# Feed-forward stage: squares on ScalarE, operands in PSUM, five pairs ahead, a second pair ahead in each down group, first token half finished first

## Chip, cores and metric

The kernel runs on one core of one Trainium2 chip. The metric is the device time of one execution in microseconds; the time before is the median of three runs, 2409.03 us (2401.53 to 2418.07).

## What is computed

A decoder layer over 1024 tokens of width 1024: two gated branches (a recurrent one and a dilated attention), cross-attention over 256 memory rows, a squared-ReLU feed-forward part and a final normalisation. The change touches the last two alone:

```python
u = rmsnorm(h, norm_ffn_g[l]) @ ffn_w1[l]                 # 1024 x 4096
h = h + (jnp.square(jax.nn.relu(u)) @ ffn_w2[l])
return rmsnorm(h, norm_final_g)
```

All of it is in fp32. A matmul with fp32-like precision is three matmuls: each operand is split into a high part `h` and a low remainder `l`, and `h*ah + h*al + l*ah` is summed in PSUM.

## The kernel before

Activations are kept transposed, `hT[d][half]`: 128 features by 512 tokens, two token halves. Both products of the feed-forward part are done with seven block products in place of eight (Strassen's method in Winograd's form). For an up **pair** (two blocks of 128 of the 4096 features; 16 pairs, `up_item`) the four weight blocks a0 to a3 and the sums made of them (`weights`, L1391: c3 = a2+a3, c2 = c3-a0, c4 = a0-a2, c6 = a1-c2) are multiplied with seven **combinations** of the normalised activations (`com[j]`, four pairs of tiles each). A product j is twelve matmuls of 512 columns (`seventh`, L1416) into one of four PSUM banks (`ms_tile`). `up_evac` (L1434) adds the seven results into the four blocks u11, u12, u21, u22, applies squared ReLU on VectorE (`squared`, L1428), forms the combinations that the down product needs (L1488 to L1491) and writes seven tiles per pair to DRAM (`uscr`). The down product runs in four **groups** g of 1024 features; a group has four items q (each two output blocks). At a group's first item `second` (L1539) loads the four tiles of each combination back (`ur`, six buffers, four of them shared with other tiles) and splits them: a cast on ScalarE, in three of four cases a copy of the high part into a PSUM tile (`split_psum`, `pacc`: two banks), and the low part on VectorE. `down_evac` (L1497) adds the seven results into `hT`, some of the additions on GpSimd.

A weight block is loaded by SyncE's queue (`f_raw`, six buffers), cast on ScalarE and its low half taken on GpSimd (`f_split`, L1379); four split blocks can wait for TensorE.

The seven combinations of the up product are made by `first_coms` (L1549): those of the first half (0 and 1) before the stage, 2 to 6 in the order 3, 4, 2, 5, 6 while the stage runs, on VectorE with casts on ScalarE. To have work meanwhile, `prologue` does products 0 and 1 of the first `PRO` = 3 pairs; what they give is kept in SBUF (product 0) and DRAM (the finished u11). `stream` (L1690) then goes through the items: product 0 of an item, product 5 of the previous one, product 1, product 6 of the previous one, and 2, 3, 4. Pairs of the prologue do 3, 4, 2. In the last group the outputs are finished (`finish`: four transposes, squares with a row sum on ScalarE, a multiplication by the final weight), and `last(half)` scales by the row norm and stores, 16 transfers of 256 KB on SyncE's queue. In the last item the order of the products is 2, 4, 5, 3, 6, and both calls of `last` come behind the sixth.

Each engine works through its instructions in one fixed order. The program's order is the order in which the generators above are advanced (`weave`, L151, deals steps of two streams out in proportion); the framework lays out the engines' queues at build time from that order, its own estimate of durations and the release of buffers, so an instruction whose inputs are early can stand ahead of ones that come before it in the program.

Of the kernel before, what the change touches and what calls it, by code (L numbers as in the profile page):

```python
# [41 lines left out]
def hybrid_layer(ctx, tc, x, mem, norm_mix_g, w_in, shift_mu, w0, w2, a0, a2, g2, k_k, k_a, r_k, gn_w, gn_b,  # L42
# [1336 lines left out]
    def f_split(raw):  # L1379
# [5 lines left out]
        nc.gpsimd.tensor_tensor(l, raw, h.bitcast(F32), op=ALU.subtract)  # L1385
# [5 lines left out]
    def weights(views, early=False):  # L1391
# [4 lines left out]
        def get(j):  # L1396
            if j < 2:
                return f_split(f_raw(views[j]) if early else a[j])
            if not c:
                c[3], c[2] = f_sum(), f_sum()  # L1400
                nc.vector.tensor_tensor(c[3], a[2], a[3], op=ALU.add)  # L1401
                nc.vector.tensor_tensor(c[2], c[3], a[0], op=ALU.subtract)
            if j in (2, 3):
                return f_split(c[j])
            if j == 4:
                c[4] = f_sum()
                nc.vector.tensor_tensor(c[4], a[0], a[2], op=ALU.subtract)
                w = f_split(c[4])
                c[6] = f_sum()
# [18 lines left out]
    def squared(dst, src):  # L1428
        nc.vector.scalar_tensor_tensor(dst, src, 0.0, src, op0=ALU.max, op1=ALU.mult)

    def add(dst, a, b, eng=None):
        (eng or nc.vector).tensor_tensor(dst, a, b, op=ALU.add)  # L1432

    def up_evac(p, st, j):  # L1434
# [8 lines left out]
        elif j == 1:  # L1443
            st["11"] = staged() if p >= PRO else bt.tile([P, H2], F32, tag="nt", name=nm("ua"))
            add(st["11"], st["a"], ps)
            if p >= PRO:
                squared(st["11"], st["11"])
            else:
                nc.scalar.activation(st["11"], st["11"], AF.Relu)
                nc.scalar.activation(st["11"], st["11"], AF.Square)  # L1450
            put(0, st["11"])
        elif p < PRO and j in (2, 3, 4):

            if j == 3:
                st["12"] = staged()
# [24 lines left out]
        elif j == 6:  # L1480
# [5 lines left out]
            squared(u12, u12)  # L1486
            t1, t2, t4 = [staged() for _ in range(3)]
            nc.vector.tensor_tensor(t1, u12, u11, op=ALU.subtract)  # L1488
            nc.vector.tensor_tensor(t2, u22, t1, op=ALU.subtract)
            nc.vector.tensor_tensor(u12, u22, u12, op=ALU.subtract)  # L1490
            nc.vector.tensor_tensor(t4, u21, t2, op=ALU.subtract)  # L1491
# [5 lines left out]
    def down_evac(g, q, st, j):  # L1497
        (h11, h12), (h21, h22) = [[hT[2 * q + e][half] for half in range(2)] for e in range(2)]
        ps = st["p", j]
        if j in (0, 2, 4):  # L1500
            t = staged()
            if j == 0:
                nc.scalar.copy(t, ps)
            else:
                add(t, st["t"], ps)
            st["t"] = t
        if j == 0:
            add(h11, h11, t, nc.vector)
        elif j == 1:
            add(h11, h11, ps)  # L1510
        elif j == 2:
            add(h12, h12, t, nc.gpsimd)
        if j == 4:
            add(h21, h21, t, nc.gpsimd)
            add(h22, h22, t, nc.vector)
# [224 lines left out]
```

## Time and profile before

| | us |
|---|---|
| median of three runs | 2409.03 |
| lowest, highest | 2401.53, 2418.07 |
| profiled execution | 2407.52 |
| its span, first to last instruction | 2405.8 |
| busy in the span: TensorE, VectorE, ScalarE, GpSimd | 2292.9, 1545.9, 1088.3, 889.4 |

The feed-forward stage is the last 686 us of the span (from about 1719.5 us); all matmuls of it have the lines L1422 to L1424. Matmuls are pipelined: the profile's duration of one is longer than the distance to the next, so the pace is read from counts. [...]

### The profile page before, as it was taken

What the parts mean: (1) busy time and instruction counts of PE and PEld (TensorE: products, weight loads), DVE (VectorE), ACT (ScalarE), POOL (GpSimd) and SP (SyncE); (2) the same over time, 40 slices, a digit from 0 to 9 for tenths busy, and PEclk for the clock granted to TensorE, in tenths of its full rate; (3) what the DMA queues carried; (4) which work ended last, traced back from release to release, by engine and by line L of the source; (5) the groups of instructions that cost most, each with busy time, mean ns of one, the idle gap of its engine ahead of it and who ended that gap; (6) DMA issues with size and microseconds to landing.
All of it is one profiled execution on the core that took longest, in us unless ns stands there. A gap on an engine that the chain in (4) does not pass through costs nothing. (4 is left out here: it accounts for less than half of the span.)

```text
span 2405.8 us, 47020 instructions
## 1 busy us (share of the span) xinstructions
PE 2292.9 (95%) x18645; PEld 1827.2 (76%) x18645; DVE 1545.9 (64%) x2735; ACT 1088.3 (45%) x2118; POOL 889.4 (37%) x737
## 2 busy tenths in 40 slices
PE   6999999999999999999999999999989999899997
PEld 5777777777777777777777888888768888678785
DVE  6638676786776722233474666345799898876685
ACT  5525645546455434333443445444432222565464
POOL 4321222222222223111245534423535554566664
PEclk9999999999999999999999999999999999999998
DMA  5221111111111123121245554223244444653352
GB/s 174 58 65 35 37 39 35 37 42 28 34 38 37 46 67 106 41 67 45 82 149 161 168 150 135 81 61 87 81 133 152 149 145 160 217 167 118 119 156 71
DMA packets 301619, 226.73 MB, mean 94 GB/s; under 512 B 16229, under 2 KB 252375, under 8 KB 301399
## 3 DMA queue, kind: packets, MB, share of 16 engines
q1 hardware_dynamic: 301111, 223.20, 30.6%
q8 instruction: 147, 2.41, 0.4%
q14 instruction: 73, 0.60, 0.1%
q10 hardware_dynamic: 288, 0.52, 0.1%
HBM read 169.99 MB, written 53.67 MB: 93 GB/s over the span
## 5 line engine op out<-in xcount | busy, mean ns | idle before, releaser
L143 PE MATMUL acc<-ah,wh 128*128 128x512 f32 (+1 forms) x1600 | 652.4, 408 | 8.4 <-DVE al L1266 2.9
L144 PE MATMUL acc<-al,wh 128*128 128x512 f32 (+1 forms) x1600 | 618.2, 386 | 2.8 <-POOL al L231 1.5
L145 PE MATMUL acc<-ah,wl 128*128 128x512 f32 (+1 forms) x1600 | 618.2, 386 | 0.4 <-POOL wl L112 0.4
L112 POOL TENSOR_TENSOR wl<-wr,wh 128x512 fp32r<-128x512 f32 x248 | 334.6, 1350 | 706.9 <-ACT wh L110 668.3
L143 PEld LDWEIGHTS acc<-ah,wh 128*128 128x128 f32 x1600 | 302.8, 189 | 76.3 <-issue 3.9
L145 PEld LDWEIGHTS acc<-ah,wl 128*128 128x128 f32 x1600 | 302.7, 189 | 62.5 <-POOL wl L112 1.0
L144 PEld LDWEIGHTS acc<-al,wh 128*128 128x128 f32 x1600 | 303.4, 190 | 50.9 <-POOL al L231 3.3
L110 ACT CAST wh<-wr 128x512 fp32r<-128x512 f32 (+1 forms) x296 | 179.6, 607 | 299.2 <-PE acc L144 186.1
L1423 PE MATMUL ms<-al,wh 128*128 128x512 f32 x768 | 304.5, 396 | 10.4 <-DVE al L1537 5.4
L1422 PE MATMUL ms<-ah,wh 128*128 128x512 f32 x768 | 304.4, 397 | 5.4 <-ACT ah L128 2.5
L1424 PE MATMUL ms<-ah,wl 128*128 128x512 f32 x768 | 302.3, 394 | 0.0
L1385 POOL TENSOR_TENSOR wl<-ws,wh 128x512 fp32r<-128x512 f32 x128 | 178.6, 1398 | 177.7 <-ACT wh L1384 149.6
L1385 POOL TENSOR_TENSOR wl<-sr,wh 128x512 fp32r<-128x512 f32 x96 | 140.4, 1465 | 113.7 <-ACT wh L1384 113.6
L1423 PEld LDWEIGHTS ms<-al,wh 128*128 128x128 f32 x768 | 145.2, 189 | 48.7 <-DVE al L129 9.5
L1422 PEld LDWEIGHTS ms<-ah,wh 128*128 128x128 f32 x768 | 145.1, 189 | 41.9 <-ACT ah L128 5.0
L1424 PEld LDWEIGHTS ms<-ah,wl 128*128 128x128 f32 x768 | 145.2, 189 | 31.9 <-POOL wl L1385 0.2
L1384 ACT CAST wh<-ws 128x512 fp32r<-128x512 f32 x128 | 79.0, 620 | 171.5 <-PE ms L1423 145.9
L1384 ACT CAST wh<-sr 128x512 fp32r<-128x512 f32 x96 | 59.5, 620 | 147.7 <-PE ms L1423 136.7
L937 DVE CUSTOM_DVE_ANT_0 sS<-pS,bias 128x128 f32<-128x128 f32 (+1 forms) x96 | 30.2, 349 | 113.5 <-PE pS L125 113.3
L399 ACT ACTIVATE gt<-acc 128x512 f32<-128x512 f32 x32 | 19.0, 594 | 127.1 <-PE acc L145 121.3
L942 ACT ACTIVATE sS<-sS,nm 128x128 f32<-128x128 f32 (+1 forms) x96 | 42.5, 443 | 75.2 <-DVE nm L940 72.1
L1432 DVE TENSOR_TENSOR sg<-sg,ms 128x512 f32<-128x512 f32 x70 | 47.7, 683 | 37.5 <-PE ms L1424 36.6
(420 smaller groups left out, 4048.3 us busy)
## 6 DMA issues: line engine op xcount, KB each, us to landing
sr<-in_ffn_w_dram SPq DMA_DIRECT2D x134, 256.0 KB
wr<-in_w_in_dram SPq DMA_DIRECT2D x120, 256.0 KB
ur<-uscr SPq DMA_DIRECT2D x112, 256.0 KB
uscr<-sg SPq DMA_DIRECT2D x93, 256.0 KB
gtscr<-gt SPq DMA_DIRECT2D x32, 256.0 KB
g<-gtscr SPq DMA_DIRECT2D x32, 256.0 KB
wr<-in_p_rwkv_dram SPq DMA_DIRECT2D x32, 256.0 KB
wr<-in_w_out_dram SPq DMA_DIRECT2D x32, 256.0 KB
```

Of the source, the lines that this page charges most:

```text
L110: nc.scalar.copy(h, raw)
L112: lo_eng.tensor_tensor(l, raw, h.bitcast(F32), op=ALU.subtract)
L143: mms.append(nc.tensor.matmul(ps, h, ah, start=(k == 0), stop=False))
L144: mms.append(nc.tensor.matmul(ps, h, al, start=False, stop=False))
L145: mms.append(nc.tensor.matmul(ps, l, ah, start=False, stop=(k == len(acts) - 1)))
L942: nc.scalar.activation(sS[:, h, lo:], sS[:, h, lo:], AF.Exp, bias=nm2[:, h:h + 1], scale=0.125, accum_out=Og[:, b, 130 + h:131 + h])
L1384: nc.scalar.copy(h, raw)
L1385: nc.gpsimd.tensor_tensor(l, raw, h.bitcast(F32), op=ALU.subtract)
L1422: nc.tensor.matmul(ps, h[:, k, :], ah, start=(k == 0), stop=False)
L1423: nc.tensor.matmul(ps, h[:, k, :], al, start=False, stop=False)
L1424: nc.tensor.matmul(ps, l[:, k, :], ah, start=False, stop=(k == 3))
L1432: (eng or nc.vector).tensor_tensor(dst, a, b, op=ALU.add)
```

## The change

The squares of up pairs become two ScalarE passes, Relu and Square. Weight sums c3 and c2 of the up pairs from 5 on and of the first three down groups are made in two PSUM banks (`f_psum`), and the low halves of those two are taken on VectorE; c4 becomes a3-c2, which is the same sum. The tiles b12, b2 and b of the evacuations stand in `pacc` banks, so that VectorE's sums there have one operand in PSUM, and the additions that GpSimd made in `down_evac` and `last` go to VectorE and ScalarE. `PRO` is 5; pairs 3 and 4 keep product 0 in DRAM and load it back for product 3 (`KEPT` = 3). In each down group products 0 and 1 of the second item (`ahead`) are done before products 2, 3, 4 of the first, from weight blocks loaded for that and loaded again later. In the last item (`final`) the order is 0, 5 of the item before, 1, 2, 4, 5, 6 of the item before, 3, 6, and `last(0)` stands ahead of product 6.

```diff
--- before.py
+++ after.py
@@ -1376,19 +1376,22 @@
         nc.sync.dma_start(t, ap)
         return t
 
-    def f_split(raw):
+    def f_split(raw, lo_eng=None):
         pool = wq[0] if wn[0] % 4 == 3 else wp
         wn[0] += 1
         h = pool.tile([P, 4, P], F32R, tag="wh", name=nm("wh"))
         l = pool.tile([P, 4, P], F32R, tag="wl", name=nm("wl"))
         nc.scalar.copy(h, raw)
-        nc.gpsimd.tensor_tensor(l, raw, h.bitcast(F32), op=ALU.subtract)
+        (lo_eng or nc.gpsimd).tensor_tensor(l, raw, h.bitcast(F32), op=ALU.subtract)
         return h, l
 
     def f_sum():
         return wrp[-1].tile([P, 4, P], F32, tag="wr", name=nm("ws"))
 
-    def weights(views, early=False):
+    def f_psum():
+        return fps.tile([P, 4, P], F32, tag="f", name=nm("wf"))
+
+    def weights(views, early=False, bank=False, held=False):
 
         a = [None if early else f_raw(v) for v in views]
         c = {}
@@ -1397,16 +1400,17 @@
             if j < 2:
                 return f_split(f_raw(views[j]) if early else a[j])
             if not c:
-                c[3], c[2] = f_sum(), f_sum()
+                c[3], c[2] = [f_psum() if bank else f_sum() for _ in range(2)]
                 nc.vector.tensor_tensor(c[3], a[2], a[3], op=ALU.add)
                 nc.vector.tensor_tensor(c[2], c[3], a[0], op=ALU.subtract)
             if j in (2, 3):
-                return f_split(c[j])
+                return f_split(c[j], nc.vector if bank else None)
             if j == 4:
+
                 c[4] = f_sum()
-                nc.vector.tensor_tensor(c[4], a[0], a[2], op=ALU.subtract)
+                nc.vector.tensor_tensor(c[4], a[3], c[2], op=ALU.subtract)
                 w = f_split(c[4])
-                c[6] = f_sum()
+                c[6] = staged().rearrange("p (k c) -> p k c", c=P) if held else f_sum()
                 nc.vector.tensor_tensor(c[6], a[1], c[2], op=ALU.subtract)
                 return w
             return f_split(a[3] if j == 5 else c[6])
@@ -1426,10 +1430,11 @@
                 yield
 
     def squared(dst, src):
-        nc.vector.scalar_tensor_tensor(dst, src, 0.0, src, op0=ALU.max, op1=ALU.mult)
-
-    def add(dst, a, b, eng=None):
-        (eng or nc.vector).tensor_tensor(dst, a, b, op=ALU.add)
+        nc.scalar.activation(src, src, AF.Relu)
+        nc.scalar.activation(dst, src, AF.Square)
+
+    def add(dst, a, b):
+        nc.vector.tensor_tensor(dst, a, b, op=ALU.add)
 
     def up_evac(p, st, j):
         def put(jj, t):
@@ -1441,17 +1446,18 @@
             st["a"] = bt.tile([P, H2], F32, tag="nt", name=nm("ua"))
             nc.scalar.copy(st["a"], ps)
         elif j == 1:
-            st["11"] = staged() if p >= PRO else bt.tile([P, H2], F32, tag="nt", name=nm("ua"))
+            st["11"] = staged() if p >= KEPT else bt.tile([P, H2], F32, tag="nt", name=nm("ua"))
             add(st["11"], st["a"], ps)
-            if p >= PRO:
-                squared(st["11"], st["11"])
-            else:
-                nc.scalar.activation(st["11"], st["11"], AF.Relu)
-                nc.scalar.activation(st["11"], st["11"], AF.Square)
+            if KEPT <= p < PRO:
+                put(1, st["a"])
+            squared(st["11"], st["11"])
             put(0, st["11"])
         elif p < PRO and j in (2, 3, 4):
 
             if j == 3:
+                if p >= KEPT:
+                    st["a"] = staged()
+                    nc.sync.dma_start(st["a"], uscr[(p * 7 + 1) * P:(p * 7 + 2) * P, :])
                 st["12"] = staged()
                 add(st["12"], st["a"], ps)
             elif j == 4:
@@ -1483,12 +1489,15 @@
                 nc.sync.dma_start(st["11"], uscr[p * 7 * P:(p * 7 + 1) * P, :])
             u11, u12, u21, u22 = st["11"], st["a"], st["21"], st["22"]
             add(u12, u12, ps)
-            squared(u12, u12)
+
+            b12, b2 = acc_tile(), acc_tile()
+            squared(b12, u12)
             t1, t2, t4 = [staged() for _ in range(3)]
-            nc.vector.tensor_tensor(t1, u12, u11, op=ALU.subtract)
-            nc.vector.tensor_tensor(t2, u22, t1, op=ALU.subtract)
-            nc.vector.tensor_tensor(u12, u22, u12, op=ALU.subtract)
-            nc.vector.tensor_tensor(t4, u21, t2, op=ALU.subtract)
+            nc.vector.tensor_tensor(t1, b12, u11, op=ALU.subtract)
+            nc.vector.tensor_tensor(u12, u22, b12, op=ALU.subtract)
+            nc.vector.tensor_tensor(b2, u22, t1, op=ALU.subtract)
+            nc.scalar.copy(t2, b2)
+            nc.vector.tensor_tensor(t4, u21, b2, op=ALU.subtract)
             put(3, t1)
             put(2, t2)
             put(4, u12)
@@ -1497,22 +1506,25 @@
     def down_evac(g, q, st, j):
         (h11, h12), (h21, h22) = [[hT[2 * q + e][half] for half in range(2)] for e in range(2)]
         ps = st["p", j]
-        if j in (0, 2, 4):
-            t = staged()
-            if j == 0:
-                nc.scalar.copy(t, ps)
-            else:
-                add(t, st["t"], ps)
-            st["t"] = t
         if j == 0:
-            add(h11, h11, t, nc.vector)
+            st["t"] = staged()
+            nc.scalar.copy(st["t"], ps)
+            add(h11, h11, ps)
         elif j == 1:
             add(h11, h11, ps)
         elif j == 2:
-            add(h12, h12, t, nc.gpsimd)
-        if j == 4:
-            add(h21, h21, t, nc.gpsimd)
-            add(h22, h22, t, nc.vector)
+
+            t = staged()
+            add(t, st["t"], ps)
+            st["t"] = t
+            b = acc_tile()
+            nc.scalar.copy(b, t)
+            add(h12, h12, b)
+        elif j == 4:
+            b = acc_tile()
+            add(b, st["t"], ps)
+            add(h21, h21, b)
+            add(h22, h22, b)
         if 3 in st["seen"] and 4 in st["seen"] and j in (3, 4):
             add(h22, h22, st["p", 3])
             add(h12, h12, st["p", 3])
@@ -1620,13 +1632,13 @@
         it["evac"](it["st"], j)
         yield
 
-    def item(views, evac, **kw):
-        return dict(st={}, w=weights(views), evac=evac, **kw)
+    def item(views, evac, bank=False, held=False, **kw):
+        return dict(st={}, w=weights(views, bank=bank, held=held), evac=evac, **kw)
 
     def up_item(p):
-        return item(up_views(p), lambda st, j: up_evac(p, st, j))
-
-    PRO = 3
+        return item(up_views(p), lambda st, j: up_evac(p, st, j), True)
+
+    PRO, KEPT = 5, 3
     early = []
 
     def prologue():
@@ -1657,12 +1669,11 @@
         rstd_small(rf, rf, eps_n)
         for d in range(NK):
             h = hT[d][half].rearrange("p (j c) -> p j c", j=4)
-            if d % 4 == 2:
+            if d % 8 in (2, 5, 7):
                 for j in range(4):
                     nc.scalar.activation(h[:, j, :], h[:, j, :], AF.Copy, scale=rf[:, j:j + 1])
             else:
-                (nc.gpsimd if d % 4 == 3 else nc.vector).tensor_tensor(h, h, rf.unsqueeze(2).broadcast_to([P, 4, P]),
-                                                                      op=ALU.mult)
+                nc.vector.tensor_tensor(h, h, rf.unsqueeze(2).broadcast_to([P, 4, P]), op=ALU.mult)
             nc.sync.dma_start(out2[half * H2:(half + 1) * H2, d * P:(d + 1) * P].rearrange("(j p) c -> p j c", p=P), h)
 
     gf, sf = [], [bt.tile([P, 4, 8], F32, tag="sf", name=nm("sf"), bufs=2) for _ in range(2)]
@@ -1685,35 +1696,69 @@
                         gf.append(staged())
                         nc.scalar.dma_start(gf[e], norm_final_g[e * H2:(e + 1) * H2].rearrange("(o d) -> o d", o=1)
                                             .broadcast_to([P, H2]))
-                yield item(down_views(g, q), lambda st, j, g=g, q=q: down_evac(g, q, st, j), **kw), True
+                evac = lambda st, j, g=g, q=q: down_evac(g, q, st, j)
+                if q == 1:
+                    ahead["w"] = weights(down_views(g, q), bank=g < 3)
+                    yield dict(ahead, **kw), False
+                    continue
+                it = item(down_views(g, q), evac, g < 3, g == 3 and q > 1, **kw)
+                if q == 0:
+
+                    ahead = dict(st={}, w=weights(down_views(g, 1), True), down=True,
+                                 evac=lambda st, j, g=g: down_evac(g, 1, st, j))
+                    it["ahead"] = ahead
+                yield it, True
+
+    def finishing(gen):
+
+        for i, _ in enumerate(gen):
+            if ready and i % 2:
+                finish(*ready.pop(0))
+            yield
 
     def stream():
-        prev, ready = None, []
+        prev = None
         for it, whole in items():
+            if it.get("done") == 3:
+                yield from final(prev, it)
+                return
             if whole:
                 yield from run(it, 0)
             if prev:
-                yield from run(prev, 5)
+                yield from finishing(run(prev, 5))
             if whole:
-                yield from run(it, 1)
-            if prev:
-                yield from run(prev, 6)
+                yield from finishing(run(it, 1))
+            if prev and it.get("done") != 3:
+                yield from finishing(run(prev, 6))
                 if "done" in prev:
-                    ready += [(2 * prev["done"] + e, half) for half in range(2) for e in range(2)]
-            for j in (3, 4, 2) if not whole else (2, 4, 5, 3, 6) if it.get("done") == 3 else (2, 3, 4):
-                for i, _ in enumerate(run(it, j)):
-                    if ready and i % 2:
-                        finish(*ready.pop(0))
-                    yield
-                if j == 5:
-                    ready += [(6, 0), (7, 0)]
-                if j == 6:
-                    finish(7, 1)
-                    finish(6, 1)
-                    last(0)
-                    last(1)
+                    ready.extend((2 * prev["done"] + e, half) for half in range(2) for e in range(2))
+            if "ahead" in it:
+                yield from run(it["ahead"], 0)
+                yield from run(it["ahead"], 1)
+            for j in (3, 4, 2) if not (whole or "down" in it) else (2, 3, 4):
+                yield from finishing(run(it, j))
             prev = it
 
+    def final(prev, it):
+
+        yield from finishing(run(it, 0))
+        yield from finishing(run(prev, 5))
+        ready.extend([(4, 0), (5, 0), (5, 1)])
+        for j in (1, 2, 4, 5):
+            yield from finishing(run(it, j))
+        ready.extend([(6, 0), (7, 0)])
+        yield from finishing(run(prev, 6))
+        ready.append((4, 1))
+        yield from finishing(run(it, 3))
+        ready.append((7, 1))
+        last(0)
+        yield from finishing(run(it, 6))
+        while ready:
+            finish(*ready.pop(0))
+        finish(6, 1)
+        last(1)
+
+    ready = []
     coms = first_coms(1)
     weave((chain(prologue(), stream()), 48, 0, 100), (coms, 22, 0, 90))
 _INS = ['x', 'mem', 'norm_mix_g', 'w_in', 'shift_mu', 'w0', 'w2', 'a0', 'a2', 'g2', 'k_k', 'k_a', 'r_k', 'gn_w', 'gn_b',
```

## Rows read from the trace of the kernel before

**Rows 1.** Windows: length; PE, PEld, DVE, ACT, POOL busy (count); PEclk; DMA share; GB/s.

```profile
1744.00:1787.00 43.00, 32.20 (x107) 22.18 (x108) 42.24 (x62) 15.72 (x27) 13.74 (x11) 0.88 0.36 117
1787.00:2045.00 258.00, 258.00 (x1124) 210.84 (x1123) 234.44 (x257) 67.05 (x112) 131.97 (x93) 1.00 0.47 153
2045.00:2088.00 43.00, 34.67 (x136) 24.29 (x135) 38.48 (x57) 30.03 (x55) 20.03 (x14) 1.00 0.78 247
2143.00:2168.00 25.00, 22.90 (x97) 18.10 (x98) 23.46 (x30) 16.13 (x31) 16.81 (x12) 1.00 0.63 200
2240.00:2253.00 13.00, 10.49 (x38) 7.95 (x38) 10.24 (x12) 2.33 (x5) 10.17 (x7) 0.87 0.36 108
```

**Rows 2.** Timeline of TensorE, last product, its first and last matmul: start, us.

```profile
2384.12 0.48 PE L1422 MATMUL ms<-u,wh 128*128 128x512 f32 x1
...
2386.74 0.39 PE L1424 MATMUL ms<-u,wl 128*128 128x512 f32 x1
```

**Rows 3.** Waits of TensorE, 1740 to 1790 us: total, times, longest.

```profile
PE ms L1422 <- DVE sg L1432: 3.4, 1, 3.4
```

**Rows 4.** Waits of TensorE, 2045 to 2090 us.

```profile
PE ms L1423 <- DVE al L1537: 4.1, 5, 1.3
```

**Rows 5.** Waits of SyncE's queue, 2040 to 2088 us.

```profile
SPq L1546 <- DVE al L1537: 15.5, 14, 3.3
```

**Rows 6.** Waits of TensorE, 2143 to 2330 us.

```profile
PE ms L1422 <- DVE h L1432: 3.9, 3, 2.2
```

**Rows 7.** Timeline of SyncE's queue, the output transfers' issues.

```profile
2388.62 13.32 SPq L1666 DMA_DIRECT2D out_dram<-h  x16
```

**Rows 8.** Groups of VectorE, 1725.6 to 1770 us: count, busy us, mean ns.

```profile
L129 DVE TENSOR_TENSOR al<-acc,ah 128x512 fp32r<-128x512 f32 x12 | 7.8, 682 | 0.1
...
L1598 DVE TENSOR_TENSOR acc<-b,sg 128x512 f32<-128x512 f32 x4 | 2.7, 692 | 0.0
...
L1410 DVE TENSOR_TENSOR ws<-sr,ws 128x512 f32<-128x512 f32 x2 | 1.4, 681 | 0.0
```

**Rows 9.** Groups of the whole feed-forward stage, 1719 to 2406 us.

```profile
L1385 POOL TENSOR_TENSOR wl<-ws,wh 128x512 fp32r<-128x512 f32 x128 | 178.6, 1398 | 177.7 <-ACT wh L1384 149.6 <-PE ms L1424 10.7 <-PE ms L1423 7.2
...
L1384 ACT CAST wh<-ws 128x512 fp32r<-128x512 f32 x128 | 79.0, 620 | 171.5 <-PE ms L1423 145.9 <-DVE ws L1407 6.1 <-POOL wl L1385 5.4
...
L1432 DVE TENSOR_TENSOR sg<-sg,ms 128x512 f32<-128x512 f32 x70 | 47.7, 683 | 37.5 <-PE ms L1424 36.6
L1432 POOL TENSOR_TENSOR h<-h,sg 128x512 f32<-128x512 f32 x32 | 47.2, 1476 | 14.1 <-DVE sg L1432 8.8 <-PE ms L1424 5.4
L1407 DVE TENSOR_TENSOR ws<-sr,sr 128x512 f32<-128x512 f32 x32 | 47.1, 1472 | 2.4 <-POOL wl L1385 2.4
L1429 DVE SCALAR_TENSOR_TENSOR sg<-sg 128x512 f32<-128x512 f32 x45 | 45.3, 1008 | 0.9
...
L1401 DVE TENSOR_TENSOR ws<-sr,sr 128x512 f32<-128x512 f32 x32 | 28.0, 876 | 18.6 <-DMA sr<-in_ffn_w_dram 18.4
...
L1490 DVE TENSOR_TENSOR ua<-sg,ua 128x512 f32<-128x512 f32 x13 | 21.0, 1613 | 0.0
...
L1442 ACT COPY ua<-ms 128x512 f32<-128x512 f32 x16 | 9.3, 581 | 1.9 <-PE ms L1424 1.9
...
L1450 ACT ACTIVATE ua<-ua 128x512 f32<-128x512 f32 x3 | 1.9, 631 | 0.1
```

**Rows 10.** DMA view, 2040 to 2088 us.

```profile
DMA packets 7990, 11.08 MB, mean 231 GB/s; under 512 B 667, under 2 KB 3240, under 8 KB 7986
```

**Rows 11.** Timeline of VectorE at the end: the two final reductions.

```profile
2386.25 0.17 DVE L1656 TENSOR_REDUCE rf<-sf 128x4 f32<-128x32 f32 x1
...
2392.31 0.17 DVE L1656 TENSOR_REDUCE rf<-sf 128x4 f32<-128x32 f32 x1
```

**Rows 12.** Timeline of VectorE, the first weight sums of pair 0.

```profile
1725.64 0.68 DVE L1401 TENSOR_TENSOR ws<-sr,sr 128x512 f32<-128x512 f32 x1
...
1734.27 0.68 DVE L1402 TENSOR_TENSOR ws<-ws,sr 128x512 f32<-128x512 f32 x1
```

## The prediction, made before the result was known

> **What bounds the kernel now.** I read the stretches of the feed-forward stage first. In the long steady stretch TensorE issues 1124 matmuls in 258.00 us, one per 0.2295 us, and is never idle [rows 1]; a product of twelve then takes 2.75 us. Held against that pace, 1744 to 1787 us has 107 matmuls, worth 24.6 us of its 43.00, so 18.4 us are lost; 2045 to 2088 has 136, worth 31.2 of 43.00, a loss of 11.8; 2143 to 2168 loses 2.7 and 2240 to 2253 loses 4.3 [rows 1]. Behind the last matmul at 2387.1 us [rows 2] stand 18.7 us more. These five places, about 56 us, are all that the change can shorten; the steady stretch can only get worse, for it is at the pace of the matmuls.
>
> Next the waits, place by place. In the first one VectorE is busy 42.24 of 43.00 us [rows 1], and TensorE's longest wait, 3.4 us, is for a sum that VectorE makes while reading a product out of PSUM [rows 3]; the others are for the operands of combinations 2 to 6. [...] The second place, the turn from up to down, waits for the low halves of reloaded operands [rows 4]: DMA is at 0.78 [rows 1], and SyncE's queue waits 15.5 us for the buffers that these operands leave [rows 5]. The small gaps wait for VectorE's additions into h [rows 6], so for a PSUM bank to come free. The end is a row of sixteen output transfers, first issue at 2388.62, last at 2401.9 [rows 7].
>
> **The sum is made against** the profiled execution's 2407.5 us (span 2405.8), 1.5 below the median of 2409.0 us.
>
> **Five pairs ahead.** Two more pairs put four products, 48 matmuls or 11.0 us, ahead of the first product that needs combination 3, 4 or 2. VectorE's task until combination 6 stands is 48 instructions, nine groups of which the first and the last stand in [rows 8]; at about 0.6 us from start to start these are 29 us, plus additions and weight sums. Before, TensorE had 6 products (16.5 us) to lay over that, now it has 10 (27.5 us). So the 11.0 us move under VectorE's work, and of the second stall (3.4 us [rows 3], and the half clock behind it) I take 2 us more, because the squares leave VectorE. Bounds: it could be 5, if the weight sums of pair 0, which come behind the ten products in the program, wait behind operands on VectorE and TensorE then stands before product 3; and 17, if all but a remnant goes. I take 13. What is added: four early weight loads, two stores and two loads of products 0 for pairs 3 and 4, two more loads of products 1, ten transfers of 0.26 MB at a DMA share of 0.36 [rows 1], which the matmuls hide. The transfer that brings product 0 back stands on SyncE's queue ahead of later weight loads; behind it wait VectorE's addition and one of four PSUM banks, so its delay has some products' time to hide in.
>
> **Squares on ScalarE, operands in PSUM.** In an up pair VectorE loses four squares (mean 1.01 us [rows 9]) and gains two low halves of weights. Sums of two SBUF operands now last 0.88 to 1.61 us on average, those with a PSUM operand 0.68 [rows 9]: the former stretch when GpSimd works. VectorE's 17 instructions would then be about 12 us of the 19.3 that an up pair takes, where now 234.44/258.00 is 17.5. ScalarE gets eight passes at 0.63 and a copy at 0.58: with seven casts at 0.62 and one copy it has 10.6 us of 19.3 [rows 9]. GpSimd gives away two of seven splits at 1.40. In the steady stretch none of this is worth anything, for TensorE is at its pace; it costs nothing as long as each engine keeps its 7 us of slack. A down pair exchanges two GpSimd additions (1.48 [rows 9]) for VectorE ones and gains the two splits, against shorter sums: even.
>
> Does an operand in PSUM cost more by itself? A weight sum with two SBUF operands undisturbed takes 0.681 us [rows 8], one with a PSUM operand 0.683 [rows 9]: no. [...]
>
> **Second pair ahead in each group.** Products 0 and 1 of the group's second pair go before products 2, 3 and 4 of the first, so combinations 2 to 4 get 5.5 us longer; 5 and 6 stand at the ninth and tenth product as before. What they lack at the first turn is supply: 11.08 MB in 48 us [rows 10], and the buffer of a reloaded operand is held through cast, copy and low half, which the change leaves as they are. VectorE there loses squares and stretched sums worth some 7 us and gains splits and additions of 5. Two more weight loads (0.52 MB at 247 GB/s, 2.1 us) join the fullest transfers. Bounds: minus 2.1 and plus 7.4 (at full DMA share the 43 us of transfers need 33.5; less those 2.1). I take 3. At the three later turns 7.0 us are measured lost, two of them, and the waits are for evacuation on VectorE [rows 6], which gets no additions on GpSimd to wait for; bounds minus 4 (two loads each, beside work) and plus 7; I take 3.
>
> **First token half finished first.** Now the first half's final reduction comes at 2386.25, its first transfer 2.37 us later, the second half's reduction at 2392.31 [rows 7, 11]. The last product starts at 2384.12 [rows 2]. With the first half's reduction at about that start, transfers begin at 2386.5, 2.1 us sooner; if VectorE, mostly idle there, makes it while product 3 still runs, 4.9 sooner. The sixteen issues, 13.3 us, then run on, since eight of them (6.7 us) cover the second half's reduction, 5.2 us behind the last matmul. Bounds 0 (the second half late) and 5; I take 3.5. Additions that leave GpSimd (1.48) for VectorE or ScalarE are off the way, for transfers are the bound.
>
> **Sum.** 13 + 3 + 3 + 3.5 = 22.5; 2407.5 - 22.5 = 2385.0 us.
>
> **Rivals.** *Everything goes:* the prologue gives 17, the first turn 11, the later turns 7, the end 5: 40 us, 2367. For it: VectorE is the releaser almost everywhere. Against: the first turn's DMA share.
>
> *The change doesn't fill the gap:* the added products only move the wait. Weight sums of pair 0 and the reloads stay behind VectorE's 48 instructions, the turns are bound by transfers: 5 + 0 + 0 + 3.5, so 2399. For it: VectorE at 98% in the first place, and the same 28 operands to reload. Against: now the first two weight sums of pair 0 run amid VectorE's operand work, at 1725.6 and 1734.3 us, well before product 3 [rows 12].
>
> *Lockstep on VectorE, slower:* the low halves of weights 2 and 3 leave GpSimd, which waits for nobody but ScalarE, for VectorE's in-order queue, where evacuations stand that wait for TensorE; and the sums lie in two PSUM banks, so they can't run ahead by more than a pair. If cast and low half (0.62 + 0.68 [rows 9]) of both come into the open, that is 2.6 us in each of 11 up and 12 down pairs, 60 us: 2445. It eats the gain from 1.0 us a pair, and makes 1% slower from 2.1. Against it: weight tiles run up to four products (11 us) ahead now.
>
> **Chances.** Forecast 0.48 (own range 2374 to 2397), everything 0.22, gap moved 0.21, lockstep 0.09. A measurement of this kernel tells about 1% from no change, here 24 us: 2385 is just that bound. So faster is 0.22 and half of 0.48, 0.46; same is the other half and 0.21, 0.45; slower 0.09. The range takes in the first three cases with their bounds: 2362 to 2404.
>
> **What would show it.** Five pairs: 1720 to 1790 with at most 6 us of matmul time lost, and a granted clock of 1.00 nearly throughout; a gap just before the first product 3 shows the moved wait. PSUM operands: sums at 0.6 to 0.7 us, VectorE under 70% in the steady stretch while TensorE keeps 0.2295 us per matmul; a longer pace there, with waits for the low half of weights on VectorE, is the lockstep. Turn: waits before combinations 2 to 4 gone, those before 5 and 6 still there. End: the first output issue ahead of the last matmul, and some 15 us behind that matmul. The forecast is wrong if the steady stretch loses its pace, or if the first turn gains over 7 us, for then transfers weren't what held it.

## The result, and the profile after

The changed kernel is slower: median 2431.38 us (six runs, 2428.39 to 2437.69) against 2406.43 for six runs of the kernel before; the ratio is 1.0103 [1.0085, 1.0121]. The forecast of 2385.0 missed, and the time lies above its range. The profiled execution took 2431.73 us with a span of 2430.0.

Each stretch that the prediction costed can be counted in matmuls, as it did. Windows of the changed kernel; columns as in [rows 1], which hold what answers to them (DVE is VectorE, ACT ScalarE, POOL GpSimd, SP SyncE; PEclk is the granted share of TensorE's full clock):

```profile
1744.00:1787.00 43.00, 32.87 (x126) 23.80 (x125) 42.13 (x57) 23.63 (x42) 15.62 (x12) 0.96 0.44 143
1787.00:1840.00 53.00, 51.64 (x224) 41.74 (x223) 40.77 (x59) 27.71 (x47) 21.35 (x17) 1.00 0.61 193
1840.00:2040.00 200.00, 200.00 (x871) 163.35 (x870) 122.12 (x178) 108.24 (x181) 70.40 (x53) 1.00 0.47 156
2137.00:2176.00 39.00, 32.00 (x117) 24.28 (x116) 31.08 (x51) 27.65 (x51) 6.32 (x5) 0.87 0.68 209
```

The steady stretch is as forecast: 871 matmuls in 200.00 us, 0.2296 each, with VectorE at 61%. The prologue loses 14.1 us in the first window (126 matmuls at 0.2295 are 28.9 of 43.00) and 1.6 in the second, 15.7 where it lost 18.4: a gain of 2.7. The fourth window, a later turn, had nothing like it before.

Now the four turns, at which a group starts on newly reloaded operands. Here the same count is made with the matmuls of the feed-forward products (FFN) alone. The kernel before (columns: length, TensorE busy with count, granted clock, DMA share, GB/s):

```profile
2045.00:2093.00 48.00, 39.67 (x157) 1.00 0.79 252
2134.00:2182.00 48.00, 45.86 (x197) 1.00 0.49 157
2214.00:2262.00 48.00, 45.45 (x189) 0.96 0.48 154
2297.00:2338.00 41.00, 39.59 (x168) 1.00 0.51 155
```

The changed kernel:

```profile
2040.00:2088.00 48.00, 38.45 (x139) 0.86 0.67 212
2134.00:2182.00 48.00, 40.94 (x154) 0.89 0.62 191
2224.00:2272.00 48.00, 40.69 (x162) 0.96 0.65 202
2312.00:2360.00 48.00, 40.77 (x157) 0.93 0.52 159
```

48 us have room for 209.2 matmuls. The four turns lost 12.0, 2.8, 4.6 and 2.4 us, 21.8 in all; now they lose 16.1, 12.7, 10.8 and 12.0, together 51.6. That is 29.8 us more. At the end, the span stops 17.1 us behind the start of the last matmul, before 19.1: 2.0 gained. So 2.7 + 2.0 − 29.8 = −25.1, and the two profiled executions differ by 24.2. **The whole loss lies at the turns.** What TensorE, and below it SyncE's queue, wait for at the second turn, 2135 to 2175 us (total, times, longest):

```profile
PE ms L1427 <- DVE al L1549: 2.9, 1, 2.9
PE ms L1426 <- ACT u L1546: 2.0, 1, 2.0
PE ms L1426 <- ACT ah L1546: 1.2, 1, 1.2
PE ms L1426 <- ACT wh L1384: 0.8, 1, 0.8
```

```profile
SPq L1558 <- DVE al L1549: 15.8, 9, 6.0
```

L1546 is the cast and L1549 the low half in `split_psum`; L1558 loads `ur`. Before, the later turns waited for additions into h [rows 6]; now they wait for reloaded operands, as only the first did [rows 4, 5].

**Where the operands are held** shows on ScalarE. Its timeline before, at the second turn (start, length, engine, line, operation, idle time ahead of it):

```profile
2116.22 0.62 ACT L1534 CAST ah<-ur 128x512 fp32r<-128x512 f32 x1 [0.27 <-PE ms L1424]
2116.87 0.59 ACT L1536 COPY acc<-ah 128x512 f32<-128x512 f32 x1
```

After:

```profile
2116.10 2.01 ACT L1546 CAST ah<-ur 128x512 fp32r<-128x512 f32 x3 [0.26 <-PE ms L1428]
...
2121.59 1.32 ACT L1546 CAST ah<-ur 128x512 fp32r<-128x512 f32 x2 [0.29 <-PE ms L1428]
...
2129.88 0.59 ACT L1521 COPY acc<-sg 128x512 f32<-128x512 f32 x1 [0.28 <-DVE sg L1437]
...
2135.06 0.59 ACT L1548 COPY acc<-ah 128x512 f32<-128x512 f32 x1
2136.76 0.59 ACT L1548 COPY acc<-ah 128x512 f32<-128x512 f32 x1 [1.12 <-DVE h L1437]
```

The cast is at the same place, and the copy of the high part, 0.65 us behind it before, comes 19 us behind it. In between stands the copy of `b` (L1521). VectorE at that moment:

```profile
2130.51 0.69 DVE L1437 TENSOR_TENSOR h<-h,acc 128x512 f32<-128x512 f32 x1 [0.66 <-ACT acc L1521]
2134.71 0.70 DVE L1437 TENSOR_TENSOR acc<-sg,ms 128x512 f32<-128x512 f32 x1 [3.52 <-PE ms L1428]
2135.44 1.28 DVE L1437 TENSOR_TENSOR h<-h,acc 128x512 f32<-128x512 f32 x2
2136.65 0.68 DVE L1549 TENSOR_TENSOR al<-ur,acc 128x512 fp32r<-128x512 f32 x1
```

The first line adds the first `b` of the group's last item into h, the second makes that item's second `b` from TensorE's product, and the third adds it into h twice; only then do the next group's low halves begin. `b` and the high-part copies share the two banks of `pacc`, and the second copy (2136.76) stands waiting for that addition: the wait for a bank, seen directly. The bank of the first `b` was free from 2131.20; the first copy comes 3.9 us later, behind two weight casts in ScalarE's queue, so that last piece is the queue's. The third and fourth turn show the same order, casts, copy of `b`, then high-part copies.

### The profile page after: what moved, and what is told of

It reads as the page before. It is cut to its first block, busy times and chain, and to the rows that moved or that the text cites. A ratio compares the mean times of both kernels' runs of the same rounds, so it can differ in the third digit from the quotient of the medians.

```text
span 2430.0 us, 47090 instructions
## 1 busy us (share of the span) xinstructions
PE 2300.0 (95%) x18645; PEld 1832.4 (75%) x18645; DVE 1469.4 (60%) x2758; ACT 1183.2 (49%) x2280; POOL 755.9 (31%) x655
## 5 line engine op out<-in xcount | busy, mean ns | idle before, releaser
L1385 POOL TENSOR_TENSOR wl<-ws,wh 128x512 fp32r<-128x512 f32 x80 | 106.5, 1331 | 261.6 <-ACT wh L1384 261.5
L1385 POOL TENSOR_TENSOR wl<-sr,wh 128x512 fp32r<-128x512 f32 x96 | 128.2, 1337 | 191.3 <-ACT wh L1384 150.3
L1384 ACT CAST wh<-sr 128x512 fp32r<-128x512 f32 x96 | 59.6, 622 | 78.1 <-PE ms L1427 68.8
L1384 ACT CAST wh<-ws 128x512 fp32r<-128x512 f32 x80 | 49.6, 621 | 75.2 <-PE ms L1427 65.4
L399 ACT ACTIVATE gt<-acc 128x512 f32<-128x512 f32 x32 | 19.1, 595 | 127.3 <-PE acc L145 121.7
L1437 DVE TENSOR_TENSOR h<-h,ms 128x512 f32<-128x512 f32 x96 | 64.0, 684 | 17.4 <-PE ms L1428 15.7
```

The source lines that it names most:

```text
L1384: nc.scalar.copy(h, raw)
L1385: (lo_eng or nc.gpsimd).tensor_tensor(l, raw, h.bitcast(F32), op=ALU.subtract)
L1437: nc.vector.tensor_tensor(dst, a, b, op=ALU.add)
```

## The experiments

Theory A: `b` in `pacc` makes the split of reloaded operands wait for the last products of the item before. Rival B: the order with a second pair ahead, or its additional loads, crowds the turns. Rival L, from the prediction's lockstep: low halves and sums of weights on VectorE and in two banks. (The expectations also name a theory C: an operand in PSUM, or the way through ScalarE, costs by itself.) Every kernel below computes the whole layer. The expectations call the kernels e1, e2 and so on; these names stand in the headings. Ratios are against runs of the kernel before on the same chip, with 95% intervals; between kernels that ran on different chips a difference of ratios says more than one of medians.

A trace allows a finer count. The stage has 2688 FFN matmuls in every kernel; *late* below is the start of the n-th, counted from the first, less n times 0.2295 us. The stage itself began between 1717.9 and 1726.3 us in these traces, which this count leaves out. There is one trace of each kernel, so a difference of a microsecond or two in it may be chance. Over the four groups the kernel before becomes later by 10.7, 3.1, 5.1 and 7.4 us, the changed kernel by 15.9, 12.9, 11.1 and 17.5; the last group's figures hold the output's transposes too.

**`b` back in SBUF (e1).** From the changed kernel; the line stands twice in `down_evac`:

```diff
-            b = acc_tile()
+            b = staged()
```

> The changed kernel with the two tiles b of the down evacuation in SBUF in place of the two PSUM banks of pacc; all else as changed. Theory A (the banks are granted in the program's order, so the copies that split the next group's reloaded operands wait for the last product of the item before, 18 us after their casts): the copies start right behind the casts again at the three later turns, the loss there falls from about 28 us to under 10, time 2402 to 2414 us; the first turn, where the up pairs' b12 and b2 hold the same banks, gains little. Theory B (the second pair ahead: four weight reloads stand ahead of operand loads on SyncE's queue and the transfers double up): the turns stay as they are, 2424 us or more.

2408.28 us, 0.9995 [0.9979, 1.001]: 23.1 of the 25.0 us are back by the medians, all by the ratio, as A has it. ScalarE at that turn:

```profile
2122.20 0.62 ACT L1546 CAST ah<-ur 128x512 fp32r<-128x512 f32 x1 [0.26 <-PE ms L1428]
2122.85 0.59 ACT L1548 COPY acc<-ah 128x512 f32<-128x512 f32 x1
```

The copy follows its cast directly again, here and at the two turns after. By groups this kernel becomes later by 14.1, 1.8, 1.3 and 13.7 us: the second and third turn are healed, the last is not. What is left there depends on the weight sums, as the last run shows.

**Without the second pair ahead (e2).** From the changed kernel:

```diff
-                if q == 1:
-                    ahead["w"] = weights(down_views(g, q), bank=g < 3)
-                    yield dict(ahead, **kw), False
-                    continue
...
-                    it["ahead"] = ahead
```

> The changed kernel without the second pair ahead in a group (the order of products and the loads of the kernel before, in the first three groups; PSUM tiles as changed). Theory A: the operands are as late as before and have 5.5 us less cover, so 2428 us or more, up to 2450. Theory B: the turns lose no more than in the kernel before, 2398 to 2408 us.

2427.0 us, 1.0071 [1.0052, 1.009], just under A's bound and 19 above B's: the order costs 4 us of the loss by the medians, 8 by the ratios. That it costs at all is against A, which expected 2428 us or more for want of cover. The collision stays without it: at the second turn the casts start at 2119.77, the copy of `b` stands at 2133.55 and the first high-part copy at 2138.74.

**The new `down_evac` in the kernel before (e3)**, all else old (with it go the GpSimd additions that it replaces):

> The kernel before with the changed down evacuation alone (b in the PSUM banks of pacc, additions off GpSimd). Theory A: the copies of the reloaded operands wait for the previous item here too, three turns lose some 8 us each more, 2425 to 2445 us. Theory B: within 1% of the kernel before.

2431.11 us, 1.0086 [1.0065, 1.0108]. This one function makes a loss as large as the whole change's. Its ScalarE:

```profile
2122.59 2.01 ACT L1537 CAST ah<-ur 128x512 fp32r<-128x512 f32 x3 [0.26 <-PE ms L1424]
...
2136.37 0.59 ACT L1512 COPY acc<-sg 128x512 f32<-128x512 f32 x1 [0.28 <-DVE sg L1432]
...
2141.55 0.58 ACT L1539 COPY acc<-ah 128x512 f32<-128x512 f32 x1
```

The same picture: casts, then the copy of `b`, and only then the copies of the high parts, 18 us late.

**The second pair ahead in the kernel before (e4)**, all else old:

```diff
+                if q == 0:
+                    ahead = dict(st={}, w=weights(down_views(g, 1), True), down=True,
+                                 evac=lambda st, j, g=g: down_evac(g, 1, st, j))
+                    it["ahead"] = ahead
...
+            if "ahead" in it:
+                yield from run(it["ahead"], 0)
+                yield from run(it["ahead"], 1)
```

> The kernel before with the second pair ahead alone. Theory A: the order by itself costs nothing, 2398 to 2412 us, and TensorE's waits at the first turn shrink. Theory B: the turns lose about 25 us more, 2425 us or more.

2414.37 us, 1.0021 [1.001, 1.0033]: 2.4 above A's range, far below B's. The order costs 5.6 us there, and that small cost A did not foresee. The first group doesn't gain (late by 11.1 us against 10.7); of the 5.0 us that the stage gets longer 3.4 fall in the last group. Why is not shown.

**The prologue's own wait (e5).** In the changed kernel, TensorE's waits from 1740 to 1840 us:

```profile
PE ms L1426 <- ACT ua L1447: 4.1, 2, 3.1
PE ms L1426 <- ACT wh L1384: 3.2, 1, 3.2
```

L1447 is the copy of product 0 out of its PSUM bank, into one of the `nt` buffers. With `b` in SBUF, pairs 3 and 4 got buffers of their own for it:

```diff
-            st["a"] = bt.tile([P, H2], F32, tag="nt", name=nm("ua"))
+            st["a"] = (bt.tile([P, H2], F32, tag=("ssq", "rs")[p - KEPT], name=nm("ua"), bufs=1) if KEPT <= p < PRO else
+                       bt.tile([P, H2], F32, tag="nt", name=nm("ua")))
```

> e1 (b in SBUF) with product 0 of pairs 3 and 4 in two buffers of its own (free ones of the norm), not in the four that the other pairs' results hold. If TensorE's 3.1 us before the first product 3 is a PSUM bank that waits for such a buffer, that gap goes and the prologue gains 3 to 5 us: 2403 to 2406. If VectorE's operand work is what the prologue waits for anyway, the gap moves to combinations 5 and 6 and the time stays within 2 us of e1's 2408.

2410.06 us, 1.0017 [1.0002, 1.0031], 1.8 above the kernel with `b` in SBUF by the medians, 5 by the ratios; no gain in either. The wait for `ua` is gone and a longer one stands before a later product (same view, 1740 to 1795 us):

```profile
PE ms L1426 <- ACT wh L1384: 6.3, 1, 6.3
```

The buffer decided only where TensorE waits. In that kernel VectorE is busy 39.86 of 43.00 us between 1752 and 1795.

**A pair ahead only in the second and third groups (e6)**, `b` in SBUF:

```diff
-                if q == 1:
+                if q == 1 and g in (1, 2):
...
-                if q == 0:
+                if q == 0 and g in (1, 2):
```

> e1 with the second pair ahead in groups 1 and 2 only. By e1's and the kernel before's product starts, the order ahead costs 2 us at the first turn and 5.6 at the last and gains 1 to 4 at the two between; without it at both ends 2400 to 2404 us. If the other changes are what costs there, no difference from e1's 2408.

2405.91 us, 0.9998 [0.9985, 1.0011]: above the expected 2400 to 2404, and not told apart from the kernel with all groups.

**`b` in another PSUM bank, weight sums of down groups in SBUF (e7):**

```diff
-            b = acc_tile()
+            b = fps.tile([P, H2], F32, tag="f", name=nm("fb"))
...
-                    ahead["w"] = weights(down_views(g, q), bank=g < 3)
+                    ahead["w"] = weights(down_views(g, q), bank=False)
...
-                it = item(down_views(g, q), evac, g < 3, g == 3 and q > 1, **kw)
+                it = item(down_views(g, q), evac, False, g == 3 and q > 1, **kw)
```

> The changed kernel with b still in PSUM, but in the two banks of the other pool, whose weight sums go back to SBUF and GpSimd in the down groups. If it is the sharing of pacc's two banks with the copies of the operand split that costs (theory A), the three later turns are as good as in e1: 2402 to 2416 us. If a PSUM operand or the evacuation's way through ScalarE costs by itself (theory C), 2424 us or more.

2400.11 us, 0.997 [0.9953, 0.9988], below the range that A gave. ScalarE:

```profile
2110.66 0.59 ACT L1521 COPY fb<-sg 128x512 f32<-128x512 f32 x1 [0.28 <-DVE sg L1437]
...
2116.16 0.62 ACT L1546 CAST ah<-ur 128x512 fp32r<-128x512 f32 x1 [0.26 <-PE ms L1428]
2116.82 0.59 ACT L1548 COPY acc<-ah 128x512 f32<-128x512 f32 x1
```

`b` still lies in PSUM and is still summed by VectorE, and the copies are on time: it is the shared pair of banks, not PSUM, so theory C falls. Two things are changed at once here, though, so the gain below A's range stayed open until the last run.

**The last two up pairs off `pacc` (e8)**, `b` in SBUF; pairs 14 and 15 make their sums as the kernel before does, after squares on ScalarE:

```diff
+            if p >= 14:
+                squared(u12, u12)
+                t1, t2, t4 = [staged() for _ in range(3)]
+                nc.vector.tensor_tensor(t1, u12, u11, op=ALU.subtract)
...
+                return
             b12, b2 = acc_tile(), acc_tile()
```

> e1 with b12 and b2 of the last two up pairs in SBUF. By theory A the first turn has the same fault as the later ones had, the banks held in the program's order until product 6 of pair 15 is evacuated, so the first copies come earlier and the first turn gains 3 to 8 us: 2400 to 2405. If the first turn is bound by its transfers, nothing: 2408.

2402.0 us, 0.9985 [0.9969, 1.0002]: 6.3 less than with `b` alone in SBUF by the medians, 2.4 by the ratios; the intervals of the two ratios overlap, so the traces must tell. FFN matmuls of 60 us at the first turn (columns as above, weight loads, VectorE and ScalarE added), `b` alone in SBUF:

```profile
2034.00:2094.00 60.00, 53.36 (x199) 39.21 (x198) 12.12 (x18) 1.17 (x2) 0.91 0.73 233
```

With the last two up pairs off `pacc` as well:

```profile
2034.00:2094.00 60.00, 55.12 (x227) 42.80 (x227) 13.24 (x20) 1.14 (x2) 0.97 0.75 239
```

28 matmuls more, 6.4 us: over the whole first group 8.3 us of lateness in place of 14.1. ScalarE shows the same collision: with `b` alone in SBUF the first cast of the turn starts at 2035.53 and the first copy 8.5 us behind it, waiting at its end for the sum that reads b12's bank (L1497):

```profile
2044.03 0.59 ACT L1548 COPY acc<-ah 128x512 f32<-128x512 f32 x1 [0.23 <-DVE ua L1497]
```

With the last two pairs off `pacc` the copy (2032.99) is 1.1 us behind its cast (2031.92).

**Both edits together (e10)** (the other bank, sums in SBUF, last up pairs off `pacc`):

> e7 (b in the other pool's banks) with b12 and b2 of the last two up pairs in SBUF, as in e8. Theory A: both gains add, 2400 minus 5 to 7: 2393 to 2396 us, faster than the kernel before by about half a per cent. If what e8 gained at the first turn was chance, 2400.

2390.99 us, 0.9931 [0.9918, 0.9945], 2 under the expected range. Matmuls of its turns:

```profile
2030.00:2082.00 52.00, 47.98 (x199) 1.00 0.80 256
2128.00:2176.00 48.00, 47.00 (x205) 1.00 0.52 163
2206.00:2254.00 48.00, 48.00 (x211) 1.00 0.53 167
2285.00:2333.00 48.00, 46.32 (x199) 1.00 0.39 123
```

The later three lose 1.0, nothing and 2.3 us; the first, at a DMA share of 0.80, still loses 6.3 of 52; what holds it now was not tested. Three kernels vary this one.

*Low halves of combination 4 on GpSimd (e11)* (`split(*com[4][i], b12[i], nc.gpsimd)` for `split_psum`):

> e10 with the four low halves of combination 4 on GpSimd (and so without the four copies of their high parts). If VectorE's work until combination 6 is what the prologue waits for, four of its 48 instructions fewer give 2 to 4 us: 2390 to 2393. If GpSimd's 1.3 to 1.5 us in place of 0.68 hold combination 4 up, or stretch VectorE's sums, 0 to 4 us more than e10.

2389.86 us, 0.9927 [0.9914, 0.994]; 1.1 us less with overlapping intervals, so inconclusive.

*No pair ahead (e13):*

> e10 without the second pair ahead in a group. If the order ahead hides the operands' preparation once the banks are free, 5 to 15 us slower than e10: 2400 to 2410. If it brings nothing, as e2 against the changed kernel suggests, within 3 us of e10.

2392.14 us, 0.9934 [0.992, 0.9947]: 1.2 us more than with it, within the noise. In the two traces the first group becomes 9.4 us late without it and 6.7 with it, and the stretch from the first FFN matmul to the last is 2.8 us longer. So once the banks are free, the order brings 1 to 3 us if anything.

*Three pairs in the prologue (e14):*

```diff
-    PRO, KEPT = 5, 3
+    PRO, KEPT = 3, 3
```

> e10 with three pairs ahead in place of five. By the product starts of the changed kernel five pairs are worth 3 to 5 us, so 2397 to 2400. If VectorE bounds the prologue with either number, less than 2 us.

2393.58 us, 0.9938 [0.9925, 0.9952]. By the medians five pairs are worth 2.6 us, between the two expectations, and the intervals overlap. The prologue with three pairs (columns as in [rows 1]):

```profile
1744.00:1790.00 46.00, 37.93 (x134) 25.85 (x133) 43.77 (x67) 26.05 (x46) 18.07 (x14) 0.89 0.40 128
```

And with five:

```profile
1744.00:1790.00 46.00, 36.02 (x140) 26.49 (x139) 45.04 (x63) 25.17 (x45) 18.03 (x13) 0.96 0.47 150
```

In both VectorE has no slack (43.77 and 45.04 of 46.00), and the difference is six matmuls, 1.4 us.

**`b` in SBUF again, sums in SBUF, last up pairs off `pacc` (e15).** It differs from the kernel with the last up pairs off `pacc` only in where the weight sums of the down groups lie and which engine takes their low halves:

```diff
-                    ahead["w"] = weights(down_views(g, q), bank=g < 3)
+                    ahead["w"] = weights(down_views(g, q), bank=False)
...
-                it = item(down_views(g, q), evac, g < 3, g == 3 and q > 1, **kw)
+                it = item(down_views(g, q), evac, False, g == 3 and q > 1, **kw)
```

> e10 with b in SBUF in place of the other PSUM pool; it differs from e8 (2402) in one thing, the weight sums of the down groups: here in SBUF with low halves on GpSimd, there in two PSUM banks with low halves on VectorE. If those sums are what costs e8 its 11 us against e10 (the lockstep rival: sums that can't run ahead, low halves in VectorE's queue), 2390 to 2394. If b in SBUF costs them (sums of two SBUF operands stretched by GpSimd), 2399 to 2404.

2388.69 us, 0.9933 [0.991, 0.9956], the lowest median of all, 0.7% below the kernel before. It is 13.3 us less than 2402.0 from this one edit (12.5 by the ratios): in the traces the stretch from the first FFN matmul to the last is 649.1 us against 661.0. Windows of all matmuls over the later turns, sums in PSUM:

```profile
2125.00:2320.00 195.00, 190.80 (x830) 155.29 (x828) 168.46 (x237) 121.61 (x223) 73.06 (x53) 1.00 0.52 163
```

Sums in SBUF:

```profile
2125.00:2320.00 195.00, 194.31 (x856) 158.99 (x855) 160.25 (x227) 122.58 (x249) 98.55 (x71) 1.00 0.51 160
```

26 matmuls more fit into the same time, with GpSimd busier by 25 us and VectorE by 8 less. Only ten of the 26 are FFN matmuls (840 against 830); the others are transposes of outputs, which this kernel reaches sooner. With the sums in PSUM ScalarE waits there for weight sums of VectorE (total, times, longest; 2085 to 2350 us):

```profile
ACT wh L1384 <- DVE ws L1411: 8.2, 4, 3.6
```

L1411 is c4, which is made from c2 and lies in SBUF in both kernels. Lateness tells where the 11.9 us are: with the sums in PSUM 8.3, 1.3, 1.7 and 13.6 us over the four groups, in SBUF 6.5, 0.0, 0.0 and 7.9, and 1.4 us of difference stand already before the first group. So the three groups that the edit changes give 4.8 us and the last one 5.7, though its own sums lie in SBUF in both kernels; the longest of the four waits, 3.6 us at 2319.28, is there. The edit's gain is shown; how it reaches the last group is not.

That `b` is in SBUF here and in another bank at 2390.99 makes no difference that shows.

## Why the prediction was wrong

**The step that failed** is the sentence "A down pair exchanges two GpSimd additions (1.48 [rows 9]) for VectorE ones and gains the two splits, against shorter sums: even", and the 3 us of gain taken for the later turns need it. It priced the instructions of `b` and not the bank that they stand in. `pacc` has two banks; `b` takes one until VectorE has added it into h, which waits for a product on TensorE, and the next group's high-part copies, ready much earlier, come behind it. So the first copy starts 18 us later (2116.87 before, 2135.06 after), the `ur` buffers stay full, SyncE's queue waits, and the operands reach TensorE late. The turns were forecast to gain 6 us and lost 30 more, 4.1 at the first and 25.7 at the later three. The place was named in the text: the buffer is "held through cast, copy and low half, which the change leaves as they are". The operations stayed as they are; the banks that the copy needs did not. This is shown by taking `b` out of `pacc` (−23 us), by putting the new function alone into the kernel before (+22), and by another bank, in which `b` lies in PSUM and costs nothing that shows. At the first turn b12 and b2 of the last up pairs held the same banks. That the banks are given out in the order in which the program asks for them is read from four traces, not measured by itself.

**The rival on the other side** had the right engine and the wrong place and size. *Lockstep* priced 60 us over 23 pairs; in up pairs the pace did not change (0.2296 us), but in the down groups the sums in two banks with low halves on VectorE do cost 13 us once the first cause is gone (2402.0 against 2388.7). Half of that falls in the last group, where there are no such sums, so the rival's mechanism, cast and low half coming into the open in each pair, is not what was seen. That "weight tiles run up to four products (11 us) ahead now", the argument against it, held in the up pairs; where VectorE splits reloaded operands too, the edit did cost time.

**Five pairs ahead:** 13 us forecast, 2.7 in the trace for pairs and relief together; 2.6 by the runs with three and five, 1.4 by their traces. Failed: "So the 11.0 us move under VectorE's work". The wait moved on instead, as the rival *gap moved* has it, with its sign before product 3: 3.1 us for the copy of product 0, and, when that was taken away, 6.3 before a later product. The half clock counted into the 2 us is in the trace before, granted 0.50 from 1782.9 to 1786.3 us behind the wait of 3.4 us [rows 3]; in the changed kernel it is 0.50 from 1778.1 to 1781.5, behind a wait of 3.2 us for a weight cast (L1384). The check "at most 6 us lost" failed with 14.1 to 15.7. VectorE was at 98% before and is at 98% after [rows 1]. It lost 5.3 us of squares there, but sums of two SBUF operands took longer beside GpSimd, among them these (VectorE's groups from 1744 to 1787 us, the changed kernel):

```profile
L1604 DVE TENSOR_TENSOR acc<-sg,b 128x512 f32<-128x512 f32 x4 | 4.8, 1232 | 0.0
L1610 DVE TENSOR_TENSOR acc<-b,sg 128x512 f32<-128x512 f32 x4 | 3.8, 965 | 0.0
L1411 DVE TENSOR_TENSOR ws<-sr,ws 128x512 f32<-128x512 f32 x2 | 3.3, 1638 | 0.0
```

In the same window before, these three had means of 692, 692 and 680 ns; the difference is 5.2 us, as much as the squares had taken. The five of them that lasted 1.52 us or more all began while a GpSimd subtraction was running; the other five lasted 0.69.

**Squares on ScalarE, operands in PSUM:** right. In the steady stretch of the changed kernel (VectorE's groups, count, busy, mean ns):

```profile
L1498 DVE TENSOR_TENSOR acc<-sg,sg 128x512 f32<-128x512 f32 x14 | 19.0, 1357 | 0.0
...
L1496 DVE TENSOR_TENSOR sg<-acc,sg 128x512 f32<-128x512 f32 x14 | 9.7, 692 | 19.7 <-ACT acc L1434 19.7
L1404 DVE TENSOR_TENSOR wf<-sr,sr 128x512 f32<-128x512 f32 x12 | 9.3, 774 | 1.0 <-DMA sr<-in_ffn_w_dram 0.6
```

An operand in PSUM leaves the sum at 692 ns, 11 ns above the 681 of an undisturbed sum with two operands in SBUF [rows 8]. Two in SBUF have a mean of 1357 in one group and 774 in another: ten of the twelve sums at L1404 had no GpSimd instruction beside them and lasted 0.70 us, while the fourteen at L1498 all had one and lasted 0.69 to 1.82. The gain, however, falls in a stretch where TensorE sets the pace.

**Second pair ahead:** a gain of 6 us was forecast over the turns. By itself it cost 5.6 in the kernel before and 4 to 8 in the changed one, and it gained 1.2, within the noise, once banks and sums were out of the way. Why it costs is not shown.

**First half first:** mechanism right (the first output issue at 2412.59, ahead of the last matmul at 2412.92), size off: 2.0 us of 3.5. Behind that matmul's end the span has 16.7 us where it had 18.7, and not some 15. The first half's final reduction is done at 2408.82, but the step after it on VectorE comes only at 2411.66, behind work on the other half:

```profile
2412.59 13.58 SPq L1677 DMA_DIRECT2D out_dram<-h  x16
```

## What to carry to other kernels

Before a tile is moved into an existing PSUM pool, list who else takes banks from that pool and what each holder waits for; here banks whose release waited for TensorE held up the next group's requests by 18 us. Moving work off a busy engine pays only where that engine is what the bounding one waits for; here it took 30 points off VectorE's load (91% to 61%) in a stretch at TensorE's pace and none at the saturated place. When a change of several parts loses, put its parts alone into the old kernel: one function made the loss, and with `b` and the last up pairs out of the shared banks and the down groups' sums back in SBUF the rest gained 0.7%.

## What was not expected of the hardware

A few short gaps cost more than themselves: in the changed kernel's second turn the four waits listed are 6.9 us, while 117 matmuls in 39.00 us are a loss of 12.1; the granted clock there averages 0.87, for it is 0.50 from 2157.0 to 2163.8 us and from 2170.6 to 2174.1, and the missing 0.13 of 39.00 us is 5.1 us, which with the 6.9 makes up the loss. The clock falls where TensorE was busy 1.84 of 5.00 us (2155 to 2160, granted 0.70); in the next 5.00 us, all busy, it is 0.62 and 15 matmuls are counted where 22 fit. In the kernel with both turns freed, the same turn shows 1.00.
